# Weight casts and the head gate moved from ScalarE and VectorE to GpSimd in the attention stage of a hybrid streaming encoder

## The chip, the cores and the metric

The kernel runs on one core of one Trainium2 chip. The time is device microseconds of one execution. In the text and in the rows of the profile PE is the matmul engine (TensorE), PEld its weight loads, DVE is VectorE, ACT is ScalarE, POOL is GpSimd and SP is SyncE, which here issues the transfers. Each engine works through its own instructions in order and waits for others by semaphores.

## What is computed

One inference step of one layer, on 1024 frames of a new stream and 32 frames of a running stream with 512 cached frames (1056 columns together), in fp32:

```python
h = rmsnorm(x, norm_g)
q = rmsnorm(h @ Wq, q_g) * HEAD_DIM ** -0.5      # 16 heads of 64
k = rmsnorm(h @ Wk, k_g); v = h @ Wv
logf = log_sigmoid(h @ Wf + b_f)
u = (h @ Wua) * sigmoid(h @ Wub)
ga, gb, ma, mb = h @ Wga, h @ Wgb, h @ Wma, h @ Wmb
# A: causal softmax attention, logit[t,s] = q.k + C[t] - C[s], C = cumsum(logf)
o = softmax(q @ k.T + bias, causal) @ v
# B: causal depthwise conv of width 31
conv = causal_dwconv(u, w_dw) + b_dw
ya = (o * silu(ga)) @ w_pa
yb = (silu(layernorm(conv, ln_g, ln_b)) * silu(gb)) @ w_pb
y = x + (sigmoid(ma) * ya + sigmoid(mb) * yb) @ w_out
```

Keys, values, forget gates and the last 30 conv rows are outputs too.

## The kernel before

Channels lie on the 128 partitions and the 1056 frames along the free axis. A projection of 128 output channels is a *group*: three chunks of 352 columns, eight contraction tiles each. Products are made in split precision: a weight tile `raw` (128 x 1024 fp32) is scaled and cast to a high part `wh` in fp16 (`Batch.high`, line 138, on ACT), the rest is the low part `wl` (`Batch.low`, line 141, on DVE, in three pieces), and one contraction tile takes three matmuls, `wh*xh`, `wl*xh`, `wh*xl` (line 183). Such a triple is one *step*, and after each step `beat` (line 199) advances a *tick* and starts what is due at it.

Weights come in pairs of groups, so that a pair lasts 48 ticks. `begin` (line 221) makes the table of due ticks for the next pair: squares of both weights on ACT (3 and 13), a sum over partitions on PE (`total`, 25), the power-of-two scale on DVE (`power`, 27, with a small POOL instruction for its inverse, line 135), the cast of the first weight at 29 with its lows at 30, 32, 34, and the second at 39 with lows at 40, 42, 44.

The stages follow one another: input split and the first conv projections, values, queries and keys with the remaining conv projections, the `ga` gates, then **attention** from about 555 to 1055 us, then the projections `pa`, `pb` and `out`. The 31 taps of the depthwise conv are sums on DVE (line 371) spread over the ticks; the last ones fall into the attention stage.

Attention goes through 16 heads of 8 query blocks, with four pieces for the running stream put between them. In the slot of block n the code issues: the scores of block n+3 (lines 1121 and 1122, PE; causal mask 1124 and row maximum 1126, DVE); the transposes of the probabilities of block n (`turn`, line 1153, PE, into one of two PSUM banks `psT`; copied out at line 1156 by ACT for the first four tiles and by DVE for the others); the exponential of block n+3 (1133, ACT); the normalization of block n+2 (reciprocal 1138 on DVE, product 1139 on POOL, in place in `P`); two *fill steps* of a gate projection `gb`, `ma` or `mb`; in the slot of block 1 the value products of the head before (1172, PE, into both `psT` banks); two more fill steps. After the value products ACT copies one half (1176) and DVE adds the other (1177), and for odd heads DVE multiplies by the gate `ga` (1179), which came by a transfer; then SP stores `ot`. There are 528 fill steps for 132 slots; 12 go ahead of the first slot, and the first three blocks of head 8 get none (line 1258).

Once all conv sums are in, one step of `layernorm` goes out per slot: the mean, then for each of three chunks the mean square on PE (`over_channels`), ACT's square of the mean, and DVE's difference (1216), then the inverse root.

The orders of PE, DVE, ACT and SP in this stage are as the code issues them. POOL's order there is set by the scheduler of the framework, by when it reckons an instruction can run.

Of the kernel before, what the change touches and what calls it, by code (L numbers as in the profile page):

```python
# [8 lines left out]
F32 = mybir.dt.float32  # L9
# [8 lines left out]
D = 1024  # L18
T = 1024
# [34 lines left out]
def build(tc, xT, xt, wv, wf, ckT, cv, clT, stT, vec, cst, yT, kT, vO, lfO, cpT, csT):  # L54
# [35 lines left out]
    class Batch:  # L90
# [44 lines left out]
            nc.gpsimd.tensor_scalar(self.inv, q, back, 1.0, op0=ALU.mult, op1=ALU.mult)  # L135

        def high(self, i, wh, raw, ks):
            nc.scalar.mul(wh[:, ks, :], raw[:, ks, :], self.s[:, i:i + 1])  # L138

        def low(self, i, wl, wh, raw, ks):  # L140
# [45 lines left out]
    def csl(c):  # L186
        return slice(c * CH, (c + 1) * CH)
# [33 lines left out]
    def begin():  # L221

        if not plan:
            return
        b = plan.pop(0)
        after = plan[0] if plan else None
        t = pace["tick"]
        jobs = [(25, b.total), (27, b.power)]
        if b.keys[0] == ("v", 0):
            jobs = [(32, b.total), (33, b.power), (10, lambda: b.stage(0)), (17, lambda: b.stage(1)),  # L230
                    (34, lambda: split.__setitem__(b.keys[0], split_v(0, b)))]
        elif b.n == 2:
            jobs += [(3, lambda: b.stage(0)), (13, lambda: b.stage(1))]
            for i, n in ((0, 29), (1, 39)):
                jobs.append((n, lambda i=i: b.split(i)))
                jobs += [(n + 1 + 2 * p, lambda i=i, p=p: b.rest(i, p)) for p in range(3)]
        else:
            jobs += [(3 + 10 * i, lambda i=i: b.stage(i)) for i in range(2)]
            jobs.append((29, lambda: split.__setitem__(b.keys[0], split_v(b.keys[0][1], b))))
        if after:  # L240
            jobs += [(5 + 10 * i, after.load) for i in range(after.n)]
        prep.extend((t + n, fn) for n, fn in sorted(jobs, key=lambda e: e[0]))
# [115 lines left out]
    def sums(f):  # L358
        return [lambda: from_shift(f, sides["y", f]), lambda: into_sums(f, sides["y", f])]
# [637 lines left out]
    pe = ExitStack()  # L997
    pe.enter_context(tc.manual_schedule(engines={E.PE, E.SP, E.DVE, E.Activation}))
    pace["rate"], pace["credit"] = R_A, 0.0
    taps.extend(sums(7))  # L1000
    psS = pool("psS", 2, stack=p2, space=PS)
    psT = pool("psT", 2, stack=p2, space=PS)
# [20 lines left out]
    def fill(n):  # L1023
        for _ in range(n):
            next(flow, None)
# [78 lines left out]
    class Block:  # L1104
# [53 lines left out]
        def values(self):  # L1158
            if self.i == 5 and self.head.h % 2:
                self.head.g = ap.tile([128, T], F32, name="ga", tag="kc", bufs=1)  # L1160
                nc.sync.dma_start(self.head.g, s_g["ga"][self.head.h // 2, :, :T])
            if self.i < 7:
                return
            e, V, ot, parts = self.head.h % 2, self.head.V, self.head.ot, self.head.p
            own = slice(64 * e, 64 * e + 64)
            oth = slice(64 - 64 * e, 128 - 64 * e)
            pos = [psT.tile([128, 512], F32, name="po", tag="T") for _ in range(2)]
            for c in range(4):
                po = pos[c // 2][:, 256 * (c % 2):256 * (c % 2) + 256]
                for j in range(2 * c + 2):  # L1170
                    rows = slice(64 * (j % 2), 64 * (j % 2) + 64)
                    nc.tensor.matmul(po[rows], V[:, j, :], parts[c][:, j, :], start=(c % 2 == 0 and j < 2),  # L1172
                                     stop=(c % 2 == 1 and j >= 2 * c))
            for u in range(2):
                sl = slice(512 * u, 512 * u + 512)
                nc.scalar.copy(ot[own, sl], pos[u][oth])
                nc.vector.tensor_add(ot[own, sl], ot[own, sl], pos[u][own])
                if e == 1:
                    nc.vector.tensor_mul(ot[:, sl], ot[:, sl], self.head.g[:, sl])
            if e == 1:  # L1180
                nc.sync.dma_start(s_o[self.head.h // 2, :, :T], ot)

# [16 lines left out]
    def over_channels(acc, put):  # L1199
        for c in range(3):  # L1200
            pm = psT.tile([128, 512], F32, name="psn", tag="T")
            nc.tensor.matmul(pm[:, :CH], ones_f, acc[:, csl(c)], start=True, stop=True)
            put(csl(c), pm[:, :CH])
            yield

    def layernorm():
# [3 lines left out]
            yield  # L1210
        yield from over_channels(mean, lambda sl, ps: nc.scalar.mul(mean[:, sl], ps, 1.0 / D))

        def put(sl, ps):
            t = t352("t", 3)
            nc.scalar.activation(t, mean[:, sl], AF.Square)
            nc.vector.scalar_tensor_tensor(rstd[:, sl], ps, 1.0 / D, t, op0=ALU.mult, op1=ALU.subtract)
            nc.vector.tensor_add(mean[:, sl], mean[:, sl], shift[:, sl])
            nc.vector.tensor_scalar(rstd[:, sl], rstd[:, sl], EPS, None, op0=ALU.add)

        yield from over_channels(rstd, put)  # L1220
        for c in range(6):
            sl = slice(c * CH // 2, c * CH // 2 + CH // 2)
            v, y = rstd[:, sl], t352("t", 3)[:, :CH // 2]
# [20 lines left out]
    for n, b in enumerate(seq):  # L1244
# [10 lines left out]
            seq[n + 3].soft()  # L1255
        if n + 2 < len(seq):
            seq[n + 2].norm()
        some = 2 if isinstance(b, Sample) or b.i > 2 or b.head.h != 8 else 0
        fill(some)
        if n >= 2 and pending(seq[n - 2]):  # L1260
            seq[n - 2].values()
        fill(some)
        if n >= 3 and isinstance(seq[n - 3], Sample):
            seq[n - 3].finish()
        if "ready" in sides:
# [403 lines left out]
```

## Time and profile before

| | us |
|---|---|
| median of 3 runs | 1348.63 (1346.65 to 1349.82) |
| the profiled execution's own time | 1345.89 |
| its span | 1344.1 |
| PE busy | 1312.6 (98%) |
| DVE busy | 990.4 (74%) |
| ACT busy | 719.0 (53%) |
| POOL busy | 505.8 (38%) |

Rows of the profile give for a group of instructions the line, engine, operation, output<-inputs, shapes and count, then the busy time, the mean in ns, and the idle time of the engine ahead of them with what ended it. Rows in order of time start with the start and the duration in us; a bracket gives the idle time ahead and the releaser. Ends of matmuls are modelled, so a wait of PE is somewhat longer than its idle time.

### The profile page before, as it was taken

The page shows a single profiled execution, that of the slowest core. Times are in us where ns is not written, and L with a number is a line of the kernel's source. Part 1 is how long each engine was busy: PE and PEld are TensorE (multiplying, and loading weights), DVE is VectorE, ACT ScalarE, POOL GpSimd, SP SyncE. Part 2 cuts the span into 40 slices and gives each one's busy share as a digit, 9 for nine tenths or more (in the row PEclk, how much of TensorE's full clock was granted, in tenths as well). Part 3 has the DMA queues.
Part 4 walks back from the last instruction along what each step waited for, and adds up shares of the span by engine and source line. Part 5 has one row for each costly group of instructions (what it writes and reads, how often), then busy time and mean ns, then how long its engine had stood idle before and what let it go on. Part 6 is the DMA issues. An engine that isn't in the chain of part 4 may idle for free.

```text
span 1344.1 us, 24837 instructions
## 1 busy us (share of the span) xinstructions
PE 1312.6 (98%) x9383; PEld 1003.1 (75%) x9383; DVE 990.4 (74%) x1532; ACT 719.0 (53%) x1362; POOL 505.8 (38%) x548
## 2 busy tenths in 40 slices
PE   8999999999999999999889998999999999999999
PEld 5687876666666666667567766777776699999998
DVE  6797879888999997987778866655554489166664
ACT  6644555757676743455555555655555566233320
POOL 2001124547484820243433442222222158255562
PEclk8999999999999999999999999999999999999999
DMA  6343233425352463535644643565452698544462
GB/s 251 98 140 104 93 112 118 139 82 187 95 180 87 162 166 109 160 90 155 165 109 123 186 132 99 147 179 132 131 152 54 240 313 262 176 128 146 142 190 69
DMA packets 113496, 194.97 MB, mean 145 GB/s; under 512 B 34080, under 2 KB 80032, under 8 KB 113376
## 3 DMA queue, kind: packets, MB, share of 16 engines
q1 hardware_dynamic: 113232, 193.31, 46.9%
q8 instruction: 74, 1.21, 0.4%
q14 instruction: 46, 0.38, 0.1%
q10 hardware_dynamic: 144, 0.07, 0.0%
HBM read 127.68 MB, written 65.64 MB: 144 GB/s over the span
## 4 chain that ended last, share of the span: by engine, by line
PE 82%; DVE 9%; ACT 3%; issue 2%; DMA 2%; SPq 1%; POOL 0%; DVEq 0%; ACTq 0%; POOLq 0%
PE pj L183 56%; PE pjv L761 6%; PE pj L1501 6%; PE po L1172 4%; PE ptr L1153 3%; DVE nm L1126 2%; DVE wl L141 2%; DVE y L371 2%; PE psS L1122 2%; PE psS L1121 2%; DMA ga<-s_ga 2%; ACT wh L138 1%; DVE psS L1124 1%; DMA s_q<-qh 1%; PE warm L477 1%
## 5 line engine op out<-in xcount | busy, mean ns | idle before, releaser
L183 PE MATMUL pj<-xh,wh 128*128 128x352 f16 (+2 forms) x1536 | 481.6, 314 | 2.3 <-ACT wh L138 1.4
L183 PE MATMUL pj<-xh,wl 128*128 128x352 f16 (+2 forms) x1536 | 481.2, 313 | 0.7 <-DVE wl L141 0.6
L183 PE MATMUL pj<-xl,wh 128*128 128x352 f16 (+2 forms) x1536 | 480.9, 313 | 0.5 <-DVE xl L579 0.4
L183 PEld LDWEIGHTS <-wh 128*128 128x128 f16 x3072 | 301.5, 98 | 162.1 <-issue 7.1
L371 DVE SCALAR_TENSOR_TENSOR y<-u,vec_t,y 128x1086 f32<-128x1086 f32 x240 | 346.8, 1446 | 12.0 <-ACT y L368 8.9
L1139 POOL TENSOR_SCALAR P<-P,nm 128x128 f32<-128x128 f32 (+7 forms) x128 | 129.9, 1015 | 279.9 <-DVE nm L1138 229.8
L183 PEld LDWEIGHTS <-wl 128*128 128x128 f16 x1536 | 150.5, 98 | 72.0 <-DVE wl L141 1.6
L141 DVE SCALAR_TENSOR_TENSOR wl<-raw,sc,wh 128x384 f16<-128x384 f32 (+1 forms) x192 | 128.2, 693 | 48.3 <-ACT wh L138 48.3
L1133 ACT ACTIVATE P<-psS,nm 128x128 f32<-128x128 f32 (+7 forms) x128 | 95.1, 743 | 113.3 <-DVE nm L1138 70.9
L1126 DVE TENSOR_REDUCE nm<-psS 128x1 f32<-128x128 f32 (+7 forms) x128 | 97.0, 758 | 12.5
L1153 PE MATMUL ptr<-ident,P 128*128 128x128 f32 x576 | 88.6, 276 | 17.3 <-DVE pt L1156 9.2
L175 POOL TENSOR_TENSOR wl<-raw,wh 128x384 fp32r<-128x384 f32 (+1 forms) x51 | 63.3, 1270 | 74.3 <-ACT wh L172 58.6
L1153 PEld LDWEIGHTS ptr<-ident,P 128*128 128x128 f32 x576 | 69.2, 141 | 28.2 <-DVE pt L1156 12.1
L1156 ACT COPY pt<-ptr 128x512 f32<-128x512 f32 (+3 forms) x128 | 64.3, 502 | 44.4 <-PE ptr L1153 43.2
L1121 PE MATMUL psS<-KB,QB 128*128 128x256 f32 (+2 forms) x192 | 81.8, 427 | 0.6 <-ACT P L1133 0.6
L880 POOL TENSOR_TENSOR sql<-sqf,sqh 128x352 fp32r<-128x352 f32 x48 | 57.0, 1187 | 65.8 <-ACT sqh L877 65.8
L138 ACT ACTIVATE wh<-raw,sc 128x1024 f16<-128x1024 f32 (+1 forms) x68 | 73.9, 1091 | 8.2 <-DVE sc L158 7.9
L1172 PE MATMUL po<-pt,V 128*64 128x256 f32 x640 | 72.8, 382 | 2.5 <-ACT pts L1078 1.7
L1124 DVE TENSOR_TENSOR psS<-psS,cmask 128x128 f32<-128x128 f32 x128 | 37.6, 294 | 46.0 <-PE psS L1122 45.6
L906 POOL TENSOR_TENSOR ql<-qn,qh 128x352 fp32r<-128x352 f32 (+1 forms) x48 | 67.8, 1429 | 6.6 <-ACT qh L905 6.5
L761 PE MATMUL pjv<-vwh,xh 128*128 128x260 f16 x256 | 70.1, 274 | 0.0
L761 PE MATMUL pjv<-vwl,xh 128*128 128x260 f16 x256 | 70.0, 273 | 0.0
(271 smaller groups left out, 2532.9 us busy)
## 6 DMA issues: line engine op xcount, KB each, us to landing
raw<-wf SPq DMA_DIRECT2D x92, 512.0 KB
QB<-s_q SPq DMA_DIRECT2D x32, 256.0 KB
KB<-s_k SPq DMA_DIRECT2D x32, 256.0 KB
kT<-qn SPq DMA_DIRECT2D x8, 528.0 KB
s_ga<-t SPq DMA_DIRECT2D x24, 176.0 KB
s_gb<-t SPq DMA_DIRECT2D x24, 176.0 KB
s_ma<-t SPq DMA_DIRECT2D x24, 176.0 KB
s_mb<-t SPq DMA_DIRECT2D x24, 176.0 KB
```

The costliest lines, as they stand in the source:

```text
L138: nc.scalar.mul(wh[:, ks, :], raw[:, ks, :], self.s[:, i:i + 1])
L141: nc.vector.scalar_tensor_tensor(wl[:, ks, :], raw[:, ks, :], self.s[:, i:i + 1], wh[:, ks, :], op0=ALU.mult, op1=ALU.subtract)
L183: nc.tensor.matmul(ps, a[:, kt, :], b(kt, sl), start=(first and n == 0), stop=(last and n == N - 1))
L371: t = nc.vector.scalar_tensor_tensor(y, u[:, i:i + CW], w, y, op0=ALU.mult, op1=ALU.add)
L761: nc.tensor.matmul(ps[:, :VC], a, b, start=(n == 0), stop=(n == 23))
L1121: nc.tensor.matmul(ps[:, b, :wm], QB[:, qsl], KB[:, ksl], start=True, stop=False)
L1126: nc.vector.tensor_reduce(nm[:, 0:1], ps[:, :nb, :w], axis=AX.XY, op=ALU.max, negate=True)
L1133: nc.scalar.activation(P[:, :nk].rearrange("p (b w) -> p b w", b=nb), ps[:, :nb, :w], AF.Exp, bias=nm[:, 0:1], accum_out=nm[:, 1:2])
L1139: nc.gpsimd.tensor_scalar(P[:, :nk], P[:, :nk], nm[:, 2:3], 1.0, op0=ALU.mult, op1=ALU.mult)
L1153: nc.tensor.transpose(pt[:, 128 * j:128 * j + 128], P[:, 128 * (4 * u + j):128 * (4 * u + j) + 128], ident)
L1172: nc.tensor.matmul(po[rows], V[:, j, :], parts[c][:, j, :], start=(c % 2 == 0 and j < 2), stop=(c % 2 == 1 and j >= 2 * c))
L1501: nc.tensor.matmul(pss[c][:, :HC], a[:, k, :], x, start=(not more and kt == 0 and n == 0), stop=(kt == 3 and n == 2), skip_group_check=more)
```

## The change

In the attention stage `Batch.high` issues its cast on POOL; 22 casts leave ACT. `begin` then puts the total at tick 23 and the power at 24, the casts at 25 and 34, and the three lows of each 6, 8 and 10 ticks behind its cast (31, 33, 35 and 40, 42, 44). The product with `ga`, 16 instructions of 128 x 512, moves from DVE to POOL. In `layernorm` ACT's square of the mean is issued one step ahead of the matmul and the difference that uses it. The twelve steps that head 8's first three blocks do without are given to them, and block 6 of heads 2 to 13 gets three steps instead of four. PE's instructions are the same in number and kind.

```diff
         def high(self, i, wh, raw, ks):
+            if sides.get("cast") == "pool":
+                nc.gpsimd.tensor_scalar(wh[:, ks, :], raw[:, ks, :], self.s[:, i:i + 1], 1.0, op0=ALU.mult, op1=ALU.mult)
+                return
             nc.scalar.mul(wh[:, ks, :], raw[:, ks, :], self.s[:, i:i + 1])
...
             jobs += [(3, lambda: b.stage(0)), (13, lambda: b.stage(1))]
-            for i, n in ((0, 29), (1, 39)):
+            lag = 6 if sides.get("cast") == "pool" else 1
+            for i, n in ((0, 29), (1, 39)) if lag == 1 else ((0, 25), (1, 34)):
                 jobs.append((n, lambda i=i: b.split(i)))
-                jobs += [(n + 1 + 2 * p, lambda i=i, p=p: b.rest(i, p)) for p in range(3)]
+                jobs += [(n + lag + 2 * p, lambda i=i, p=p: b.rest(i, p)) for p in range(3)]
+            if lag > 1:
+                jobs[:2] = [(23, b.total), (24, b.power)]
...
     pace["rate"], pace["credit"] = R_A, 0.0
+    sides["cast"] = "pool"
     taps.extend(sums(7))
...
                 if e == 1:
-                    nc.vector.tensor_mul(ot[:, sl], ot[:, sl], self.head.g[:, sl])
+                    nc.gpsimd.tensor_mul(ot[:, sl], ot[:, sl], self.head.g[:, sl])
...
-        def put(sl, ps):
+        for c in range(3):
+            sl = csl(c)
             t = t352("t", 3)
             nc.scalar.activation(t, mean[:, sl], AF.Square)
-            nc.vector.scalar_tensor_tensor(rstd[:, sl], ps, 1.0 / D, t, op0=ALU.mult, op1=ALU.subtract)
+            yield
+            pm = psT.tile([128, 512], F32, name="psn", tag="T")
+            nc.tensor.matmul(pm[:, :CH], ones_f, rstd[:, sl], start=True, stop=True)
+            nc.vector.scalar_tensor_tensor(rstd[:, sl], pm[:, :CH], 1.0 / D, t, op0=ALU.mult, op1=ALU.subtract)
             nc.vector.tensor_add(mean[:, sl], mean[:, sl], shift[:, sl])
             nc.vector.tensor_scalar(rstd[:, sl], rstd[:, sl], EPS, None, op0=ALU.add)
-
-        yield from over_channels(rstd, put)
...
-        some = 2 if isinstance(b, Sample) or b.i > 2 or b.head.h != 8 else 0
-        fill(some)
+        fill(2)
         if n >= 2 and pending(seq[n - 2]):
             seq[n - 2].values()
-        fill(some)
+        fill(1 if getattr(b, "i", 0) == 6 and 2 <= b.head.h < 14 else 2)
```

The order of the changed program's instructions on POOL and DVE is shown in the prediction at the places that it speaks of, beside that of before.

## The prediction

> **What bounds the kernel now.** I read the page's busy shares first, then the stretches in 50 us steps, then who PE (the matmul engine) waited for in the attention stage.
>
> ```profile
> PE 1312.6 (98%) x9383; PEld 1003.1 (75%) x9383; DVE 990.4 (74%) x1532; ACT 719.0 (53%) x1362; POOL 505.8 (38%) x548
> 605.00:655.00 50.00, 46.26 (x338) 33.13 (x333) 38.19 (x73) 29.83 (x59) 22.20 (x24) 1.00 0.59 164
> 805.00:855.00 50.00, 45.33 (x302) 32.31 (x301) 30.47 (x75) 28.16 (x65) 11.70 (x23) 0.97 0.50 131
> 955.00:1005.00 50.00, 49.99 (x360) 36.81 (x361) 26.46 (x64) 27.67 (x60) 12.42 (x24) 1.00 0.51 138
> ```
>
> A stretch row gives its length, then the busy time of PE, PEld, DVE, ACT and POOL, then the granted clock. PE is the bound; the change removes no matmul, so it can only win back PE's holes: 3.7 us in 605 to 655, 4.7 us in 805 to 855 (where the clock also fell to 0.97), none in 955 to 1005. The waits of PE between 560 and 1060 us (total, times, longest):
>
> ```profile
> PE ptr L1153 <- DVE pt L1156: 9.2, 11, 1.7
> PE ptr L1153 <- ACT pt L1156: 6.4, 5, 2.2
> PE po L1172 <- ACT pts L1078: 1.7, 2, 0.9
> PE ptr L1153 <- DVE ot L1177: 1.2, 1, 1.2
> PE po L1172 <- ACT mean L1211: 0.7, 1, 0.7
> PE psS L1121 <- ACT P L1133: 0.6, 2, 0.4
> PE psn L1202 <- ACT pt L1156: 0.6, 1, 0.6
> ```
>
> Together 20.4 us. 15.6 of them are one wait: a transpose of P needs one of the two psT banks, and the bank is not yet copied out (`pt`, line 1156). Why are the copies late? Two places in order of time (start, us, engine and line; ACT and DVE ahead of the late transposes), the last of the ten waits counted below, and a line of DVE's waits:
>
> ```profile
> 587.48 1.14 ACT L138 ACTIVATE wh<-raw,sc 128x1024 f16<-128x1024 f32 x1
> 588.64 0.62 DVE L141 SCALAR_TENSOR_TENSOR wl<-raw,sc,wh 128x384 f16<-128x384 f32 x1 [2.12 <-ACT wh L138]
> 591.57 0.41 DVE L1156 COPY pt<-ptr 128x256 f32<-128x256 f32 x1
> 592.04 0.55 PE L1153 MATMUL ptr<-ident,P 128*128 128x128 f32 x3 [1.74 <-DVE pt L1156]
> ...
> 831.78 1.14 ACT L138 ACTIVATE wh<-raw,sc 128x1024 f16<-128x1024 f32 x1
> 833.64 0.58 ACT L1156 COPY pt<-ptr 128x512 f32<-128x512 f32 x1
> 834.27 0.33 PE L1153 MATMUL ptr<-ident,P 128*128 128x128 f32 x1 [2.20 <-ACT pt L1156]
> ...
> 1038.39 0.33 PE L1153 MATMUL ptr<-ident,P 128*128 128x128 f32 x1 [1.04 <-ACT pt L1156]
> DVE wl L141 <- ACT wh L138: 32.5, 20, 2.2
> ```
>
> The weight cast `wh` stands in ACT's order ahead of a `pt` copy, or the first low `wl` makes DVE stand for the cast (20 times, 32.5 us) with its own `pt` copy behind. Going through the sixteen waits, ten start within 5 us of a cast; the first is at 592.04 and the last at 1038.39, and they hold 11.4 of the 15.6 us.
>
> **Head 8.** Its first three blocks have no fill steps now (rows in order of time, then a stretch):
>
> ```profile
> 821.92 0.69 DVE L1179 TENSOR_TENSOR ot<-ot,ga 128x512 f32<-128x512 f32 x1 [2.85 <-DMA ga<-s_ga]
> 822.64 0.69 DVE L1177 TENSOR_TENSOR ot<-ot,po 64x512 f32<-64x512 f32 x1
> 823.48 0.52 PE L1153 MATMUL ptr<-ident,P 128*128 128x128 f32 x3 [1.25 <-DVE ot L1177]
> 824.57 0.86 PE L1202 MATMUL psn<-rstd,ones_f 128*128 128x352 f32 x2 [0.57 <-ACT pt L1156]
> 820.00:830.00 10.00, 8.18 (x40) 5.42 (x37) 6.34 (x14) 3.40 (x7) 1.01 (x2) 0.83 0.34 100
> ```
>
> With nothing to fill, PE reaches the transposes early, while DVE stands 2.85 us for the DMA of `ga` with the bank's second half behind it. The stretch 820 to 830 has a granted clock of 0.83, so 10 x 0.17 = 1.7 us lost to the clock beside the two waits (1.2 + 0.6).
>
> **The change part by part.**
>
> *Casts to POOL.* ACT loses 22 casts of 1.14 us (25 us), DVE the stand behind them: `wl` now comes six ticks after its cast instead of one. I count the ten waits as gone, -11.4 us; the other waits of that kind (4.2 us) I leave, since they stand behind DVE's tap sums and `P` work, and the 1.7 us for the running streams' `pts` too. The bounds of this term are 0 and -15.6.
>
> What is late next is POOL. It normalizes P for every block, and the program's order puts both casts of a pair in one piece ahead of a normalization. POOL at heads 6 and 7, before:
>
> ```order
> L1139 TENSOR_SCALAR P<-P,nm 128x640
> L135 TENSOR_SCALAR sc<-sc,back 128x2
> L1139 TENSOR_SCALAR P<-P,nm 128x768
> L1139 TENSOR_SCALAR P<-P,nm 128x896
> L1139 TENSOR_SCALAR P<-P,nm 128x1024
> ```
>
> and now, at the same place:
>
> ```order
> L1146 TENSOR_SCALAR P<-P,nm 128x640
> L135 TENSOR_SCALAR sc<-sc,back 128x2
> L139 TENSOR_SCALAR wh<-raw,sc 128x1024 x2
> L1146 TENSOR_SCALAR P<-P,nm 128x768
> L1146 TENSOR_SCALAR P<-P,nm 128x896
> ```
>
> So the second cast, written nine ticks after the first, runs right behind it. The place in the trace of before, in order of time, then two POOL rows in other states and two groups with their mean in ns, for the price of a cast:
>
> ```profile
> 764.19 0.27 POOL L135 TENSOR_SCALAR sc<-sc,back 128x2 f32<-128x2 f32 x1
> 765.14 1.87 POOL L1139 TENSOR_SCALAR P<-P,nm 128x768 f32<-128x768 f32 x1 [0.68 <-DVE nm L1138]
> 768.67 0.60 PE L1153 MATMUL ptr<-ident,P 128*128 128x128 f32 x4
> 770.31 2.25 POOL L1139 TENSOR_SCALAR P<-P,nm 128x896 f32<-128x896 f32 x1 [3.30 <-DVE nm L1138]
> 804.92 1.12 POOL L1139 TENSOR_SCALAR P<-P,nm 128x1024 f32<-128x1024 f32 x1 [0.73 <-DVE nm L1138]
> L1139 POOL TENSOR_SCALAR P<-P,nm 128x1024 f32<-128x1024 f32 x16 | 21.1, 1317 | 14.7 <-DVE nm L1138 9.9 <-ACT P L1133 4.5
> L1326 POOL TENSOR_TENSOR c_l<-y,c_h 128x1056 fp32r<-128x1056 f32 x8 | 24.2, 3036 | 9.1 <-ACT c_h L1325 6.8 <-DMA s_ya<-sma 2.3
> ```
>
> No row shows this cast on POOL. The nearest is the same operation over 1024 columns with f32 out: 1.12 us alone, 1.317 in the mean. Above it lies a two-input operation with another output type, 3.04 us. I take c = 1.32 and keep 1.12 to 3.04. At the place above the casts could start at 764.46 and the 768 normalization would begin 2c - 0.68 later than now; it ends 1.66 us ahead of its transposes. So PE waits 2c - 0.68 - 1.66 = 0.3 us at c = 1.32, nothing at 1.12, 3.7 us at 3.04. Six of the eleven pairs stand ahead of a 768 or 640 normalization; the other five stand ahead of a 256 one, with the wide values slot behind it, and I count nothing there. Six times 0.3 is 1.8: +2 us (0 to +22). The casts' own readers are safe at that price: six ticks hold 18 filler matmuls and a slot's transposes.
>
> *Gate product to POOL.* DVE at head 7's values, before:
>
> ```order
> L1138 RECIPROCAL nm<-nm 128x1
> L1177 TENSOR_TENSOR ot<-ot,po 64x512
> L1179 TENSOR_TENSOR ot<-ot,ga 128x512
> L1177 TENSOR_TENSOR ot<-ot,po 64x512
> L1179 TENSOR_TENSOR ot<-ot,ga 128x512
> L1216 SCALAR_TENSOR_TENSOR rstd<-psn,t 128x352
> ```
>
> and now:
>
> ```order
> L1145 RECIPROCAL nm<-nm 128x1
> L144 SCALAR_TENSOR_TENSOR wl<-raw,sc,wh 128x256
> L1184 TENSOR_TENSOR ot<-ot,po 64x512 x2
> L1131 TENSOR_TENSOR psS<-psS,cmask 128x128
> ```
>
> The second sum, which frees the psT bank, no longer stands behind the DMA of `ga`; POOL does, with the normalization of block 4 behind it. A product on POOL is bounded by DVE's 0.69 us and by the whole 1024-column two-input row below, 2.44; half of that, 1.22, is my value. At head 8 `ga` is there at 821.92, two products end at 824.4, and the normalization starts at 826.81 now:
>
> ```profile
> L351 POOL TENSOR_TENSOR rstd<-rstd,y 128x1024 f32<-128x1024 f32 x2 | 4.9, 2441 | 1.1 <-ACT y L355 1.1
> 826.81 0.80 POOL L1139 TENSOR_SCALAR P<-P,nm 128x640 f32<-128x640 f32 x1 [5.79 <-DVE nm L1138]
> ```
>
> Even 2.44 ends it at 826.8, so 0. SP's store of `ot` waits for POOL, about 1 us longer, with `raw` loads and gate stores queued behind; the waits of PE above name no DMA: 0.
>
> *Fill steps.* Head 8 gets its twelve steps back, which hide the two waits there (1.8 us) and keep PE busy, so the clock's 1.7 us goes: -3.5 us, bounds 0 and -3.5. Twelve sixth blocks lose a step of three matmuls, 0.45 us by the 0.15 us between their starts (row pair below), and cost that only where the next transposes were about to wait: 0 to +5.4, and I take one in ten, +0.5.
>
> ```profile
> 829.34 0.31 PE L183 MATMUL pj<-xl,wh 128*128 128x352 f16 x1
> 829.49 0.31 PE L183 MATMUL pj<-xh,wh 128*128 128x352 f16 x1
> ```
>
> *The rest.* The variance's square a step ahead spares DVE a stand behind ACT off PE's path; total and power two and three ticks earlier have ten ticks behind the second square: 0 for both, hidden by the fill steps.
>
> The sum: -11.4 - 3.5 + 2 + 0.5 = -12.4 us. The profiled execution took 1345.89 us (span 1344.1), which would become 1333.5; the runs' median, 1348.63, stands 2.7 us above it and would become 1336.2. I predict 1336 for a median.
>
> **Rivals.**
>
> *Slower: the cast pair holds up the normalizations.* One mechanism at six places. Without its own term the change gains 14.4 us, so it decides at 6 x (2c - 2.34) = 14.4, c = 2.37 us. At the upper bound of 3.04 us it costs 22 and the time is about 1356. For it: the pair has become one piece, and normalizations in the first half of the stage do take up to 2.25 us (the row of 770.31). Against it: in the second half they take 1.12, and most places have more room than 1.66 us. 10%.
>
> *DVE stays held, now by POOL.* [...]
>
> ```profile
> 760.45 1.34 DVE L371 SCALAR_TENSOR_TENSOR y<-u,vec_t,y 128x1086 f32<-128x1086 f32 x1
> 592.22 1.21 POOL L1139 TENSOR_SCALAR P<-P,nm 128x1024 f32<-128x1024 f32 x1 [4.52 <-ACT P L1133]
> 592.36 2.21 DVE L371 SCALAR_TENSOR_TENSOR y<-u,vec_t,y 128x1086 f32<-128x1086 f32 x1
> L371 DVE SCALAR_TENSOR_TENSOR y<-u,vec_t,y x240: 1328/1346/3444, 54.2 to 772.7; 128x1086 f32<-128x1086 f32 x120
> ```
>
> The tap sum that began 0.14 us after POOL took 2.21 instead of 1.34 us. If each of the 22 casts blocks DVE for its whole 1.12 us, that is 24.6 of the 32.5 us that the cast on ACT costs DVE now; a quarter of the first term is left, 2.8, and the sum is -2.8 - 3.5 + 2.5 = -3.8: 1345. [...] 16%.
>
> *More than forecast.* Every wait of the list goes and nothing new comes: -20.4 - 1.7 = -22.1, 1326.5. Against it: the `pts` waits and DVE's tap work are untouched. 8%.
>
> **How the numbers follow.** Forecast 66%, alone 1331 to 1342. Under 1327 lies half of the third rival (4%), over 1347 the first and a few parts of the second (13%): the range is 1327 to 1347. Within 0.2% (2.7 us, about what a measurement of this kernel can tell from no change) means 1345.9 to 1351.3: six of the second rival's 16 and one of the first's, 7%. Slower 9%. Faster 84%: the forecast, the third rival, ten of the second.
>
> **What would show it.** Right: ACT's `pt` waits and `wl <- wh` near nothing in the list; 800 to 850 at full clock; POOL casts of 1.1 to 1.5 us; DVE with no wait for `ga`. Wrong: transposes that wait for POOL's P where none of PE's waits above does, casts over 2.4 us, or `pt` copies as late as now behind longer DVE operations.

## The result, and the profile after

The changed kernel takes 1332.23 us (median of 4 runs, 1329.82 to 1337.1) against 1347.64 for the kernel before on the same chip: a ratio of 0.988, 95% interval 0.986 to 0.990, so 13 to 19 us are gone. The profiled execution took 1331.4 us, its span 1329.6. The prediction was 1336 for the median, and 1333.5 for the profiled execution.

From the page of the changed kernel the busy shares, then the three stretches that the prediction showed (length, then busy time of PE, PEld, DVE, ACT and POOL, then the granted clock; the last two columns are the DMA engines' share and GB/s):

```profile
PE 1309.1 (98%) x9383; PEld 1003.4 (75%) x9383; DVE 979.4 (74%) x1516; ACT 698.4 (53%) x1340; POOL 559.1 (42%) x586
605.00:655.00 50.00, 47.87 (x336) 34.81 (x335) 39.68 (x75) 27.72 (x58) 27.85 (x26) 0.97 0.52 146
805.00:855.00 50.00, 50.00 (x351) 36.27 (x349) 33.37 (x81) 29.57 (x68) 19.30 (x27) 1.00 0.48 126
955.00:1005.00 50.00, 49.36 (x361) 36.22 (x358) 27.08 (x68) 25.93 (x58) 17.91 (x26) 1.00 0.48 131
```

The stretch around head 8 (805 to 855) is full and at full clock. The stretch 605 to 655 has less of a hole than before, but now it is the one with a clock of 0.97. The last fill matmul of the attention stage starts at 1059.15 instead of 1073.91 us, 14.8 us earlier; ahead of the stage and behind it the two traces agree to 0.3 us.

PE's waits in the stage (560 to 1060 us), all that the view lists of the changed kernel:

```profile
PE ptr L1160 <- DVE pt L1163: 5.0, 6, 2.0
PE ptr L1160 <- ACT pt L1163: 2.3, 3, 1.0
PE ptr L1160 <- DVE os_t L1109: 1.5, 2, 1.2
PE po L1179 <- ACT pts L1085: 1.0, 1, 1.0
```

9.8 us instead of 20.4; the waits for `pt` copies went from 15.6 to 7.3. DVE's list no longer has a wait of `wl` for `wh` (it was 32.5 us) nor one for `ga`. The wait for `ga` has gone to POOL, where it holds up no one that PE waits for. POOL's two new groups (busy time, mean in ns, then idle time ahead of them and what ended it), and the weight loads that wait for POOL's P (2.0 us before):

```profile
L139 POOL TENSOR_SCALAR wh<-raw,sc 128x1024 f16<-128x1024 f32 x22 | 24.5, 1126 | 0.0
L1186 POOL TENSOR_TENSOR ot<-ot,ga 128x512 f32<-128x512 f32 x16 | 21.6, 1348 | 31.8 <-DMA ga<-s_ga 17.3 <-DVE ot L1184 12.4 <-issue 2.1
PEld ptr L1160 <- POOL P L1146: 1.4, 2, 1.1
```

A cast on POOL takes 1.13 us, about what it took on ACT (1.14).

### The profile page after: what moved, and what is told of

Its sections match the earlier page's. It is cut to its first block, busy times and chain, and to the rows that moved or that the text cites. A ratio compares the mean times of both kernels' runs of the same rounds, so it can differ in the third digit from the quotient of the medians.

```text
span 1329.6 us, 24797 instructions
## 1 busy us (share of the span) xinstructions
PE 1309.1 (98%) x9383; PEld 1003.4 (75%) x9383; DVE 979.4 (74%) x1516; ACT 698.4 (53%) x1340; POOL 559.1 (42%) x586
## 4 chain that ended last, share of the span: by engine, by line
PE 88%; DVE 4%; DMA 2%; ACT 2%; issue 2%; SPq 1%; POOL 1%; DVEq 0%; POOLq 0%; ACTq 0%
PE pj L186 59%; PE pjv L767 6%; PE pj L1509 6%; PE po L1179 5%; PE ptr L1160 4%; PE psS L1129 2%; PE psS L1128 2%; DMA ga<-s_ga 1%; DVE wl L144 1%; DMA pf<-s_cs 1%; PE warm L483 1%; DMA s_y<-y 1%; DVE nm L1133 1%; DVE y L377 1%; PE pst L866 0%
## 5 line engine op out<-in xcount | busy, mean ns | idle before, releaser
L1146 POOL TENSOR_SCALAR P<-P,nm 128x128 f32<-128x128 f32 (+7 forms) x128 | 143.5, 1122 | 195.1 <-DVE nm L1145 176.5
L1160 PEld LDWEIGHTS ptr<-ident,P 128*128 128x128 f32 x576 | 69.2, 141 | 17.8 <-DVE pt L1163 6.7
L120 POOL CAST topb<-tops 128x2 bf16<-128x2 f32 x35 | 18.2, 519 | 136.6 <-ACT junk L117 86.7
```

Of the source, the lines that this page charges most:

```text
L1146: nc.gpsimd.tensor_scalar(P[:, :nk], P[:, :nk], nm[:, 2:3], 1.0, op0=ALU.mult, op1=ALU.mult)
L1160: nc.tensor.transpose(pt[:, 128 * j:128 * j + 128], P[:, 128 * (4 * u + j):128 * (4 * u + j) + 128], ident)
```

## The experiments

The kernels were timed in three batches, each against runs of the kernel before on the same chip; the row of the whole change is the result above. What is said of a kernel against the whole change therefore goes by the two ratios, and such a difference is uncertain by about 4 us. "Alone" is the kernel before with one part of the change, "undone" the changed kernel without one part.

| kernel | ratio to before, 95% interval | PE idle in the stage, us | lost at half clock, us |
|---|---|---|---|
| before | 1 | 21.1 | 1.7 |
| fill steps alone | 1.000 (0.999 to 1.001) | 23.2 | 6.8 |
| gate product alone | 0.998 (0.997 to 1.000) | 23.2 | 6.8 |
| casts' part alone | 0.995 (0.993 to 0.997) | 15.3 | 6.8 |
| lows' distance alone, casts on ACT | 0.9915 (0.990 to 0.993) | 14.3 | 5.1 |
| distance on ACT and gate product | 0.990 (0.988 to 0.992) | 10.1 | 3.4 |
| casts' part undone | 0.994 (0.9915 to 0.996) | 14.7 | 1.7 |
| gate product undone | 0.993 (0.991 to 0.9945) | 17.5 | 5.1 |
| square undone | 0.990 (0.988 to 0.992) | 14.2 | 3.4 |
| fill steps undone | 0.988 (0.986 to 0.990) | 12.4 | 5.1 |
| casts on POOL, lows one tick behind | 0.989 (0.987 to 0.991) | 13.7 | 1.7 |
| each cast twice on POOL | 0.990 (0.988 to 0.992) | 14.0 | 3.4 |
| casts on ACT, lows six ticks behind | 0.986 (0.9845 to 0.9875) | 9.6 | 1.7 |
| the whole change | 0.988 (0.986 to 0.990) | 9.9 | 1.7 |

The last two columns are of the one profiled execution of each kernel: the gaps of more than 0.03 us between PE's matmuls from 555 to 1080 us, and half the length of the pieces at half clock there. In all fourteen the span less these two lies between 1317.6 and 1321.3 us, so nearly all that tells the kernels apart is in the two columns. They are of one execution, though: those of the fill steps alone and of the gate product alone lie some 3 us above their kernels' medians, that of the distance on ACT and gate product 2.4 us below.

**The casts' part alone.** The casts on POOL at ticks 25 and 34, the lows six ticks behind; the rest as before.

```diff
         def high(self, i, wh, raw, ks):
+            if sides.get("cast") == "pool":
+                nc.gpsimd.tensor_scalar(wh[:, ks, :], raw[:, ks, :], ...)
+                return
...
-            for i, n in ((0, 29), (1, 39)):
+            lag = 6 if sides.get("cast") == "pool" else 1
+            for i, n in ((0, 29), (1, 39)) if lag == 1 else ((0, 25), (1, 34)):
...
+    sides["cast"] = "pool"
```

> The kernel before with one part of the change: the 22 casts on POOL, with the total and power earlier and the lows six ticks behind. Theory (the casts on ACT make the transposes wait): nearly all of the gain of the whole change, -8 to -12 us, with no wait of DVE for a cast left and PE's waits for pt copies at about half of 15.6 us. Rival (DVE stays held by POOL, and the gain of the whole change comes from the gate product and the fill steps): -1 to -4 us, DVE's tap sums longer in the mean by 0.2 us or more.

Measured: 1342.23 us, 0.9951 of before, 6.6 us. PE's two `pt` rows, beside 9.2 and 6.4 before:

```profile
PE ptr L1160 <- DVE pt L1163: 7.7, 7, 2.0
PE ptr L1160 <- ACT pt L1163: 3.4, 2, 2.4
```

DVE no longer waits for a cast. So the mechanism is there, but on its own it gives little over half of the 11.4 us that the prediction put on it. The rival's sign is missing: the tap sums of 1086 columns became longer by 0.03 us in the mean (1.385 to 1.411 us from 555 to 780 us), not by 0.2.

PE makes the same 576 transposes of P in the same order in every kernel, so a wait can be followed from kernel to kernel by the number of its transpose. Three of the ten waits that the prediction counted as gone are still there: the 141st, 249th and 303rd transpose waited 1.27, 1.01 and 2.20 us before and wait 0.71, 1.96 and 2.44 us now. The 303rd is the one that the prediction showed at 834.27 behind a cast on ACT. Here no cast is left on ACT:

```profile
829.90 0.48 PE L1160 MATMUL ptr<-ident,P 128*128 128x128 f32 x1 [2.44 <-ACT pt L1163]
```

**The casts' part undone.** The changed kernel with the casts on ACT, the old ticks and the lows one tick behind.

```diff
-            if sides.get("cast") == "pool":
-                nc.gpsimd.tensor_scalar(wh[:, ks, :], raw[:, ks, :], ...)
-                return
             nc.scalar.mul(wh[:, ks, :], raw[:, ks, :], self.s[:, i:i + 1])
...
-            lag = 6 if sides.get("cast") == "pool" else 1
...
+            for i, n in ((0, 29), (1, 39)):
...
-    sides["cast"] = "pool"
```

> The changed kernel with the casts back on ACT at their old ticks; gate product, fill steps and the square stay changed. Theory: the remaining parts are worth -3 to -5 us against the kernel before, and DVE's wait for the cast is back at some 30 us. Rival: -10 us or more, most of the whole gain.

Measured: 1339.34 us, 0.9936. Against the whole change that is 0.0058 more, or 7.8 us (give or take 4, from the two intervals). The other parts still gain 8.6 us without it, where the prediction gave them 3.0 together; that lies between the two theories. DVE's wait is back:

```profile
DVE wl L141 <- ACT wh L138: 27.3, 16, 2.2
```

**The fill steps alone.**

```diff
-        some = 2 if isinstance(b, Sample) or b.i > 2 or b.head.h != 8 else 0
-        fill(some)
+        fill(2)
...
-        fill(some)
+        fill(1 if getattr(b, "i", 0) == 6 and 2 <= b.head.h < 14 else 2)
```

> The kernel before with the twelve missing fill steps moved from head 8 to block 6 of heads 2 to 13, nothing else. Theory: -3 us (two waits of 1.8 us at head 8 and the clock's 1.7 us gone, 0.5 us for thinner blocks). Rival (steps only change place, and the thinner blocks wait as long): 0 +- 1 us. If the clock's dip comes back elsewhere, it was not head 8's.

Measured: 1349.63 us, 1.0001 (0.9987 to 1.0014). The twelve steps at head 8 bring nothing of themselves. The two waits that they were to hide (1.25 and 0.57 us) are gone, but the 303rd transpose still waits 1.62 us and the 308th, which did not wait before, 1.53. The clock's dip is gone from head 8 in this trace, but others stand at 650, 746 and 783 us, so it was not head 8's own.

**The gate product alone.**

```diff
-                    nc.vector.tensor_mul(ot[:, sl], ot[:, sl], self.head.g[:, sl])
+                    nc.gpsimd.tensor_mul(ot[:, sl], ot[:, sl], self.head.g[:, sl])
```

> The kernel before with the product with ga on POOL, nothing else. Theory: 0 to -2 us, with PE's wait of 1.25 us for the sum at head 8 gone and DVE never waiting for ga. Rival (POOL stands for ga with the normalizations behind it): +1 to +5 us, with waits of PE for POOL's P.

Measured: 1347.73 us, 0.9984 (0.9968 to 1.0000), 2.2 us, hardly apart from nothing. At head 8 the wait of 1.25 us for the second sum is gone, but the 303rd transpose, which waited 2.20 us before, waits 3.46. ACT has a cast, a gate copy and the variance's square ahead of the `pt` copy (rows in order of time):

```profile
834.58 1.14 ACT L138 ACTIVATE wh<-raw,sc 128x1024 f16<-128x1024 f32 x1
...
835.62 0.54 ACT L944 ACTIVATE t<-pj,sc 128x352 f32<-128x352 f32 x1
...
836.06 0.49 ACT L1215 ACTIVATE t<-mean 128x352 f32<-128x352 f32 x1
...
836.44 0.58 ACT L1156 COPY pt<-ptr 128x512 f32<-128x512 f32 x1
...
837.08 0.48 PE L1153 MATMUL ptr<-ident,P 128*128 128x128 f32 x1 [3.46 <-ACT pt L1156]
```

**Distance or engine?** Two kernels split the casts' part. In the first the casts stay on ACT, at the new ticks and with the lows six behind; in the second they are on POOL, with the old ticks and the lows one behind. Everything else is as in the changed kernel.

```diff
# casts on ACT, lows six ticks behind
-            if sides.get("cast") == "pool":
-                nc.gpsimd.tensor_scalar(wh[:, ks, :], raw[:, ks, :], ...)
-                return
# casts on POOL, lows one tick behind
-            lag = 6 if sides.get("cast") == "pool" else 1
...
+            for i, n in ((0, 29), (1, 39)):
```

> The changed kernel with the casts on ACT, but still at ticks 25 and 34 with the lows six ticks behind. Theory (the cast does harm in ACT's own order, ahead of a pt copy): half or more of the 7 us between the casts undone (0.9936) and the whole change (0.9878) stays lost, so 1335 to 1340. Rival (only DVE's stand for the cast did harm, and distance alone cures it): 1331 to 1334, as the whole change.

> The changed kernel with the casts on POOL at the old ticks 29 and 39, the first low one tick behind. Theory of DVE's stand: DVE waits for POOL's cast again, some 20 us or more in sum, and 4 us or more of the gain go (1336 or more). Rival (leaving ACT is all that counts): 1331 to 1334.

Measured: 1332.41 us (0.9860) with the casts on ACT, 1337.47 (0.9894) on POOL with the lows close behind. Neither can be told from the whole change (0.9878) by its interval, but the second lies above the first, by 4.6 us. PE's waits with the casts on ACT:

```profile
PE ptr L1157 <- DVE pt L1160: 5.9, 5, 1.8
PE ptr L1157 <- ACT pt L1160: 2.4, 3, 1.0
```

ACT's share, 2.4 us, is that of the changed kernel (2.3), although ACT makes all 22 casts here.

Against the casts' part undone (0.9936) each of the two differs in one thing (the gains give or take 4 us). The first has other ticks, with the casts on ACT in both: that gives 10 us, and DVE's wait for the cast falls from 27.3 to 0.6 us. The second has the casts on another engine, at the same ticks: that gives 5.7 us, and DVE's wait falls as well, to far less than the 20 us that were expected:

```profile
DVE wl L144 <- POOL wh L139: 4.1, 3, 2.2
```

So in both ways DVE's stand for the cast goes, and the time with it. Once the ticks are the new ones, taking the casts off ACT brings nothing more that can be seen; the prediction had named a cast ahead of an ACT copy as a cause of its own. Why the second kernel is 4.6 us slower than the first is seen in part only: of 4.1 us that PE is idle longer in its trace, 1.0 stands behind DVE's longest wait for a cast, at 943, and 2.1 at the 92nd transpose, which is late in five of the fourteen traces, with the casts on either engine (see the account of the rivals below).

**Each cast twice.** To price POOL's load, every cast is issued twice on POOL.

```diff
             if sides.get("cast") == "pool":
-                nc.gpsimd.tensor_scalar(wh[:, ks, :], raw[:, ks, :], ...)
+                for _ in range(2):
+                    nc.gpsimd.tensor_scalar(wh[:, ks, :], raw[:, ks, :], ...)
```

> The changed kernel with each cast done twice on POOL, so that a pair takes 4.5 us instead of 2.2. Theory of the prediction's slower rival (six normalizations stand behind the pair, 2c - 2.34 us late at c = 2.24): +13 us, 1345. Other theory (the places have more room than that one): +2 to +6 us, with PE's waits for POOL's P at most 5 us.

Measured: 1337.55 us, 0.9902; 3 us above the whole change (give or take 4). PE's list shows the mechanism of the first rival, and that it is small:

```profile
PE ptr L1161 <- POOL P L1147: 3.1, 2, 2.0
```

PE stood for a normalization at two places, not at six; its weight loads waited for one at five (5.2 us, against 1.4 at two in the changed kernel). At a cast of twice 1.25 us (the mean of the 44) the prediction's formula, 6 x (2c - 2.34), would have given 16 us: its 1.66 us of room, read at one place, was not the room of the others.

**The fill steps undone.**

```diff
-        fill(2)
+        some = 2 if isinstance(b, Sample) or b.i > 2 or b.head.h != 8 else 0
+        fill(some)
```

> The changed kernel with head 8's first blocks without fill steps again and block 6 of heads 2 to 13 full. If the fill steps are worth nothing, as alone (1.0001): 1332. If they are worth something only where the gate product no longer stands on DVE: 1335 to 1340, with PE's waits and a clock under 1.00 back between 805 and 855 us.

Measured: 1335.83 us, which would fit the second theory, but against 1351.34 for before in the same batch: 0.9881, the whole change. From 805 to 855 us the clock is 1.00 and PE idle for 1.1 us. So alone (0 us, give or take 2) and within the change (0.4, give or take 4) these steps are worth nothing that can be measured, and head 8's hole must have been closed by other parts.

**The last four** ask where the 8.6 us without the casts' part come from, when the fill steps gave 0 and the gate product 2.2.

*The distance alone:* the kernel before, casts on ACT at the new ticks, lows six behind (`sides["cast"]` only switches the ticks here; `high` is as before).

```diff
-            for i, n in ((0, 29), (1, 39)):
+            lag = 6 if sides.get("cast") == "pool" else 1
+            for i, n in ((0, 29), (1, 39)) if lag == 1 else ((0, 25), (1, 34)):
                 jobs.append((n, lambda i=i: b.split(i)))
-                jobs += [(n + 1 + 2 * p, lambda i=i, p=p: b.rest(i, p)) for p in range(3)]
+                jobs += [(n + lag + 2 * p, lambda i=i, p=p: b.rest(i, p)) for p in range(3)]
+            if lag > 1:
+                jobs[:2] = [(23, b.total), (24, b.power)]
...
+    sides["cast"] = "pool"
```

> The kernel before, with the casts left on ACT but at the earlier ticks (25 and 34, total and power at 23 and 24) and the lows dealt six, eight and ten ticks behind; gate product, fill steps and variance's square as before. Theory 'the distance is the whole of the casts' part': the DVE wait for the cast is gone from the list, and the time falls as with the casts moved to POOL alone (0.995 of before, 6.6 us): 0.993 to 0.997. Rival 'the cast's place on ACT counts too, and only the other parts hide that in the whole change': ACT's pt waits stay near the 6.4 us of before, and the ratio is 0.997 to 1.000.

Measured: 1338.97 us, 0.9915, so 11.5 us by the ratio, from a few numbers in the table of ticks. That is better than either theory expected, and better than the same with the casts on POOL (0.9951; the intervals touch). PE's and DVE's rows:

```profile
PE ptr L1157 <- DVE pt L1160: 4.0, 5, 1.2
PE ptr L1157 <- ACT pt L1160: 3.6, 3, 2.4
...
DVE wl L141 <- ACT wh L138: 1.4, 2, 0.9
```

*The square undone:* the changed kernel with ACT's square again in the step of the difference.

```diff
...
             nc.scalar.activation(t, mean[:, sl], AF.Square)
-            yield
-            pm = psT.tile([128, 512], F32, name="psn", tag="T")
-            nc.tensor.matmul(pm[:, :CH], ones_f, rstd[:, sl], start=True, stop=True)
...
+        yield from over_channels(rstd, put)
```

> The changed kernel with the variance's square issued in the same step as the difference again, as before. The other three parts put back one at a time leave 6 us unaccounted for: without the casts' part the change still gains 8.6 us, of which the gate product alone is 2.2 and the fill steps alone 0. Theory 'the square is worth nothing and the parts interact': ratio 0.986 to 0.990, as the whole change. Rival 'the square is worth the missing 6 us': ratio 0.991 to 0.993, with a wait of DVE for ACT's square of 1 us or more, three times, and a transpose behind it.

Measured: 1337.76 us, 0.9900 (0.9878 to 0.9923), at the upper end of the first theory's range: 3 us more than the whole change, give or take 4. The trace shows where the square counts. DVE's difference waits for it, and a transpose waits for the bank that the difference reads; behind the difference come the mask and the maximum, then ACT's exponential and ACT's copy, for which a second transpose waits (two places in order of time, DVE and PE):

```profile
825.65 0.53 DVE L1223 SCALAR_TENSOR_TENSOR rstd<-psn,t 128x352 f32<-128x352 f32 x1 [1.16 <-ACT t L1222]
...
826.24 0.33 PE L1160 MATMUL ptr<-ident,P 128*128 128x128 f32 x1 [0.57 <-DVE rstd L1223]
...
830.58 0.53 DVE L1223 SCALAR_TENSOR_TENSOR rstd<-psn,t 128x352 f32<-128x352 f32 x1 [1.92 <-ACT t L1222]
...
831.08 0.44 PE L1160 MATMUL ptr<-ident,P 128*128 128x128 f32 x2 [1.46 <-ACT pt L1163]
```

These two are 2.0 of the 4.3 us that PE is idle longer than in the changed kernel's trace; 2.2 more stand at the 92nd transpose, at 647 us, long before the first square. The first of the two places is the 303rd transpose, and over the fourteen traces one part alone decides whether it waits. In the seven kernels with the square in the step of the difference it waits 0.57 to 3.46 us. In the seven with the square a step ahead it does not wait at all, whether the casts are on ACT or on POOL, the gate product on DVE or on POOL, the fill steps there or not.

*The gate product undone:* the changed kernel with the product on DVE.

```diff
-                    nc.gpsimd.tensor_mul(ot[:, sl], ot[:, sl], self.head.g[:, sl])
+                    nc.vector.tensor_mul(ot[:, sl], ot[:, sl], self.head.g[:, sl])
```

> The changed kernel with the gate product on DVE again. Theory 'the gate product is what frees the bank at odd heads': DVE stands for the transfer of ga again (near 3 us at head 8), PE has a transpose behind the second sum (L1177's like) of 1 to 3 us at one or more heads, and the ratio is 0.990 to 0.994, more than the 2.2 us that it gave alone. Rival 'the fill steps cover it at head 8, as the prediction had it (gate product 0)': ratio 0.986 to 0.990.

Measured: 1341.01 us, 0.9927: within the change the product is worth 6.6 us (give or take 4), against 2.2 alone (0 to 4.3). The theory was right on the size and wrong on the path. The list has no transpose behind the second sum; where a path can be followed, it is longer. In order of time, of this kernel:

```profile
879.71 0.69 DVE L1186 TENSOR_TENSOR ot<-ot,ga 128x512 f32<-128x512 f32 x1 [2.56 <-DMA ga<-s_ga]
...
883.34 0.90 ACT L1140 ACTIVATE P<-psS,nm 128x768 f32<-128x768 f32 x1 [2.39 <-DVE nm L1145]
...
884.23 0.55 ACT L950 ACTIVATE t<-pj,sc 128x352 f32<-128x352 f32 x1
...
884.80 0.32 SPq L951 DMA_DIRECT2D s_ma<-t  x1
...
886.30 2.38 SPq L1048 DMA_DIRECT2D pf<-s_cs  x4
...
895.00 0.75 DVE L1059 SCALAR_TENSOR_TENSOR pf<-psS,cq,pf 128x512 f32<-128x512 f32 x1 [5.04 <-DMA pf<-s_cs]
...
896.88 0.55 DVE L1163 COPY pt<-ptr 128x384 f32<-128x384 f32 x1
...
897.48 0.65 PE L1160 MATMUL ptr<-ident,P 128*128 128x128 f32 x4 [2.39 <-DVE pt L1163]
```

DVE stands for `ga`, so the row maximum is late, so ACT's exponential and the gate copy `t` behind it, so SP's store of `t`, and behind that in SP's order the loads of `pf` for the next piece of the running stream. Ten microseconds later DVE stands 5.04 us for that load, with a `pt` copy behind it. The same place in the changed kernel:

```profile
874.66 0.51 SPq L951 DMA_DIRECT2D s_ma<-t  x1
...
876.39 2.12 SPq L1048 DMA_DIRECT2D pf<-s_cs  x4
...
884.37 0.75 DVE L1059 SCALAR_TENSOR_TENSOR pf<-psS,cq,pf 128x512 f32<-128x512 f32 x1 [2.79 <-DMA pf<-s_cs]
...
886.85 0.66 PE L1160 MATMUL ptr<-ident,P 128*128 128x128 f32 x4 [0.33 <-DVE pt L1163]
```

Here the load is issued 8.9 us after the values' first copy (867.46) instead of 10.5 (875.85 there), and PE waits 0.33 us instead of 2.39. These 2.1 us are what the path is shown to cost, of 7.6 us that PE is idle longer in this trace, and three kernels with the product on POOL wait 0.9 to 1.5 us at the same transpose, the 389th. Another 3.6 us stand between 643 and 650 us, where the kernel without the fill steps, with the product on POOL, is idle nearly as long. So the price of 6.6 us is measured, and most of its path is open.

*The distance on ACT and the gate product*, on the kernel before: the diffs of the two together.

> The kernel before with two parts alone: the lows dealt six ticks behind casts that stay on ACT, and the gate product on POOL; fill steps and variance's square as before. Theory 'these two are the whole gain': ratio 0.986 to 0.990, as the whole change, at half of its edits. Rival 'parts add up as they were measured alone' (6.6 + 2.2 = 8.8 us): 0.9925 to 0.9945.

Measured: 1336.58 us, 0.9902 (0.9882 to 0.9922), 13.2 us, just outside the first theory's range and about what the distance (11.5) and the product (2.2) gave alone. The kernel with the fill steps and the square as well (0.9860) is 5.7 us faster, give or take 3. Their two traces differ by 2.3 us only, so not all of it can be seen; what stands out is head 8 (rows in order of time, of this kernel):

```profile
819.48 0.48 ACT L1219 ACTIVATE t<-mean 128x352 f32<-128x352 f32 x1
...
819.99 0.52 DVE L1220 SCALAR_TENSOR_TENSOR rstd<-psn,t 128x352 f32<-128x352 f32 x1 [1.44 <-ACT t L1219]
...
820.49 0.86 PE L1206 MATMUL psn<-rstd,ones_f 128*128 128x352 f32 x2 [1.21 <-ACT pt L1160]
...
821.51 1.09 DVE L1130 TENSOR_REDUCE nm<-psS 128x1 f32<-128x896 f32 x1
...
822.70 1.01 ACT L1137 ACTIVATE P<-psS,nm 128x896 f32<-128x896 f32 x1 [2.26 <-DVE nm L1142]
...
824.52 0.58 ACT L1160 COPY pt<-ptr 128x512 f32<-128x512 f32 x1
...
825.15 0.48 PE L1157 MATMUL ptr<-ident,P 128*128 128x128 f32 x1 [2.44 <-ACT pt L1160]
```

DVE's stand for the square makes the row maximum late, that makes the exponential late, and ACT's copy stands behind the exponential. PE loses 3.65 us in two waits, the second at the 303rd transpose. In the kernel with the square ahead and the fill steps undone that transpose does not wait, and the one wait for a difference, five transposes on, is this:

```profile
830.86 0.44 PE L1160 MATMUL ptr<-ident,P 128*128 128x128 f32 x2 [0.32 <-DVE rstd L1227]
```

In both the gate product is on POOL and head 8 has no fill steps; what differs is the square and the engine of the casts, and of these, as the 303rd transpose shows over all fourteen traces, it is the square ahead that closes this part of head 8's hole. The fill steps alone do not close it: with them PE is busy for 45.79 of the 50 us from 805 to 855, and for 45.33 before. No kernel was clearly faster than the changed one; the one with the casts left on ACT (0.9860) equals it, within the intervals, without the move to POOL.

## Why the prediction was right or wrong

The time came out 4 us under the forecast; 1332 lies in the stated range and in the likeliest case's own. The forecast gain was 12.4 us, the measured one 16.4 by the ratio (13 to 19). The mechanism that carried the forecast holds in the main: DVE's copies were late because DVE stood for the casts; that stand is gone, and the waits for `pt` copies fell to half (15.6 to 7.3 us). But the sizes were placed wrongly, in four terms, and that their sum came out near is in part luck.

- **"I count the ten waits as gone, -11.4".** The casts' part is worth 7.8 us within the change and 6.6 alone. The distance by itself, on ACT, gives 11.5. The term named two ways in which a cast makes a copy late; of those the stand of DVE is the one that pays, and at the new ticks the cast's place in ACT's order pays nothing. The count by "start within 5 us of a cast" could not tell the two apart, nor from a third cause. Three of its ten waits, 4.5 us, stay when the casts go; the largest, 2.20 us at 834.27, which the prediction showed as its example on ACT, goes with the variance's square.
- **"-3.5 us" for the fill steps, hiding head 8's waits.** Mis-sized: 0, alone and within the change. The steps do hide the two waits that were counted, but alone other waits of head 8 take their place, and within the change the gate product removes the one behind DVE's sum as well, so that each covers for the other. Head 8's largest wait, at the 303rd transpose, goes with the square, and the clock's dip was not tied to head 8.
- **The gate product's 0, and "off PE's path" for the variance's square.** The first is the step that failed outright: undone, it costs 6.6 us (give or take 4). The square costs 3 (give or take 4, so by the time alone it could be 0), of which 2.0 us stand in the trace as waits of PE, and its link to the 303rd transpose is the clearest in the record. DVE's short stands looked free because no transpose was named behind them. The path goes from DVE's maximum to ACT's exponential to ACT's copy for the square, and for the product, as far as it is shown (2.1 us), over SP's order to the next `pf` load. The prediction did write that SP's store would have loads queued behind it, and then set it to 0 because PE's waits "name no DMA". A wait of PE names the last releaser only, and that was DVE, which was itself waiting for the load.
- **"+2 us" for late normalizations.** 0 within what can be measured: a cast takes 1.13 us, not 1.32, and there is more room than at the one place that was priced; doubling the casts cost 3 us. The row of a POOL operation with the same columns had the right price, 1.12, as its lower end.

The terms' errors offset: 11.4 + 3.5 was too much for the casts and the fill steps, 0 too little for the gate and the square. Undone one at a time the parts are worth 7.8 + 6.6 + 3.0 + 0.4 = 17.8 us, beside 16.4 of the whole by its ratio; alone, the casts' part, the gate product and the fill steps give 8.7 together. The square alone was not tried, and each undone price is uncertain by 4 us, so it is not shown whether the parts add up or need each other. A hint that they do need each other is the gate product alone: PE's wait for the second sum went, and the wait at the 303rd transpose grew from 2.20 to 3.46 us.

Of the rivals, the first (the pair holds up normalizations) exists at twice the load and is small. The second, DVE held by the casts on POOL, gave nothing that the time shows (0.9878 with the casts on POOL, 0.9860 on ACT). No run shows its term, DVE blocked for the whole 1.12 us of each of the 22 casts (24.6 us): from 560 to 1060 us the tap sums and the lows took 113.4 us in the changed kernel, 109.5 before. But the stretching itself is in these runs, beside another of POOL's operations. In the kernel with the gate product undone a low that takes 0.47 us elsewhere took 2.56 beside two of POOL's products, of 1024 and 32 columns, which together run 2.81:

```profile
645.37 2.81 POOL L357 TENSOR_TENSOR rstd<-rstd,y 128x1024 f32<-128x1024 f32 x2 [0.92 <-ACT y L361]
...
645.51 2.56 DVE L144 SCALAR_TENSOR_TENSOR wl<-raw,sc,wh 128x256 f16<-128x256 f32 x1
...
649.86 0.69 PE L1160 MATMUL ptr<-ident,P 128*128 128x128 f32 x2 [3.33 <-DVE pt L1163]
```

The low began 0.14 us behind the first product, which ran from 645.37 to 647.79, and ended 0.28 us after it. PE then waits 3.33 us at its 92nd transpose. In the changed kernel the low starts 0.75 us ahead of POOL's first product and takes 1.05 us, and the same transpose waits 1.16 us.

Which of the two happens does not follow the parts. In five of the fourteen traces the 92nd transpose waits 3.25 to 3.68 us: the gate product alone, the product, the square or the fill steps undone, and the casts on POOL with the lows one tick behind. In the other nine it waits 0.70 to 1.51. Each kernel has one trace, so whether one kernel does now this and now that is open; but some 2 us, as much as a part is worth, can hang on it.

As signs the prediction had asked for `wl <- wh` near nothing (gone), 800 to 850 at full clock (it is), casts of 1.1 to 1.5 us (1.13), and no wait of DVE for `ga` (none). None of the signs of the contrary case appeared. ACT's `pt` waits fell from 6.4 to 2.3 us, but did not vanish.

## What to carry to other kernels

A consumer that is dealt one tick behind its producer can make its own engine stand for it (20 times here, 32.5 us), and whatever else is in that engine's order stands with it; more distance gave as much here as moving the producer to another engine. A short stand of an in-order engine is free only if none of what follows it on that engine, over two or three engines and queues, ends at the bound one (here 2.0 us of PE's waits are shown behind the square, 2.1 behind the gate product); follow the maximum, the exponential, the store and the load behind it before writing 0. When several parts aim at the same hole, undo them one at a time as well as trying them alone, and follow one instruction by its number through all the traces: a wait that comes and goes with one part, whatever the others do, belongs to that part, and an operation that merely stands ahead of it does not.

## What the runs showed that was not expected

**A stand of about 2 us cost more than itself.** In the attention stage the granted clock fell to half for 3.41 us at a time. From the fourteen traces PE's time can be cut into pieces of 3.41 us that begin and end with those. Of the pieces in which PE stood for 1.95 us or more, all 20 were followed by a piece at half clock; of those with 1.62 to 1.95 us, about half; of all those with less, four, each itself at half clock. There are 2100 such pieces in the stretch looked at, and the pieces at half clock lie whole multiples of 3.41 us apart. It need not be one wait: 0.97 and the first part of 1.16 us were enough in the changed kernel, while its longest wait, 1.96 us at 769, fell across two pieces and cost no clock. Three places in these columns: length, PE, PEld, DVE, ACT, POOL, clock. First the changed kernel:

```profile
641.40:644.80 3.40, 1.58 (x10) 0.93 (x8) 3.30 (x5) 1.78 (x4) 3.40 (x2) 1.00 1.09 259
644.80:648.20 3.40, 3.09 (x11) 1.78 (x12) 2.77 (x8) 2.58 (x7) 3.04 (x4) 0.50 0.40 93
...
767.70:771.10 3.40, 1.92 (x14) 1.45 (x15) 3.32 (x8) 1.31 (x3) 1.39 (x1) 1.00 0.03 5
771.10:774.50 3.40, 3.40 (x25) 2.56 (x24) 3.26 (x10) 1.34 (x5) 0.02 (x1) 1.00 0.58 213
```

and the kernel with the gate product undone, where nearly the same wait fell into one piece:

```profile
773.90:777.30 3.40, 1.41 (x12) 1.08 (x12) 3.33 (x8) 1.31 (x3) 1.28 (x1) 1.00 0.00 0
777.30:780.70 3.40, 3.40 (x14) 2.16 (x12) 3.23 (x9) 1.28 (x4) 0.11 (x1) 0.50 0.58 210
```

Each such piece lost 1.7 us, half of its 3.41. The prediction saw one and tied it to head 8's missing work; in these traces it came behind every piece in which PE stood for 0.57 of it or more (1.95 of 3.41 us), and it moved as the stands moved. So the price of a part can differ by 1.7 us here with where a wait of 2 us falls.

**Left open.** Why the casts on POOL alone gave less than on ACT at the same ticks (0.9951 against 0.9915) is not settled. Nor are 3.6 of the 14.8 us by which the stage became shorter: the gaps that can be seen account for 11.2, the pieces at half clock for none, and the ends of matmuls are modelled.
